# Sample tokens' product of carried state and C: loads and products on GpSimd over the next group, row sums of 1024 columns on VectorE

## The chip, the cores and the metric

The kernel runs on one core of a Trainium2 chip. The core has a matrix engine (TensorE, PE in the profile; PEld is its loading of weights), VectorE (DVE), ScalarE (ACT), GpSimd (POOL) and SyncE (SP). Each engine runs its own instructions in order and waits for the others by semaphores. DMA transfers are started from an engine's queue, here SP's or GpSimd's. The time is the device time of one execution in microseconds; the three runs shown of the kernel before took 1125.12, 1125.15 and 1128.03 us, median 1125.15.

## The reference

One layer of a hybrid decoder is computed in float32 for two groups of tokens with the same weights: 512 tokens of a prompt, and 8 sample tokens (one new token for each of 8 sequences with a carried state). What matters here is the state-space branch. It has 32 heads of 64 channels, a state of 128 numbers for each channel, and 8 groups of B and C vectors, each shared by 4 heads. For a sample token there is one step of the recurrence:

```
h_new = exp(dt*A) * h_prev + dt * x (outer) B          per head: 64 x 128
y     = h_new . C + D * x                               sum over the 128 state numbers
```

So y needs the product of the carried state `h_prev` and C, summed over the state:

```
(h_prev . C)[b, head, p] = sum_n state_ssm[b, head, p, n] * C[b, group(head), n]
```

for 8 tokens, 2048 channels and 128 state numbers: 2 million products. The rest of y follows from it with a factor and a dot product of B and C. y is gated, normalised and projected together with the prompt's.

## The kernel before, in words

**Tiling.** Activations lie transposed: channels on the 128 partitions, 520 columns (512 prompt tokens, then the 8 sample tokens). A weight tile of 1024 x 128 makes one output tile of 128 x 520, called a column here (`column`, L142). For accuracy each float32 operand is split in a high and a low part, `hi` by ScalarE (L116) and `lo` by VectorE (L117), and each block is multiplied three times (`product`, L124, matmuls on L129). A column's result stands in a pair of PSUM banks, `m`; there are two such pairs, so the column after the next needs the first pair emptied.

**The order of the work.** A list of steps is filled with `todo` and worked off by `perform`; the steps follow one another in the program. TensorE runs its instructions in this order (`manual_schedule` names PE alone). For the other engines and for the DMA queues a planner orders the instructions: among those whose inputs it believes to be ready it takes the one with the earliest place in the program, and what stands under `urgent()` gets a place 300 earlier. The order that it makes is fixed in the program; on the chip each queue is worked off in order.

**The scan.** For each of 8 groups g come four columns (`x0`, `x1`, `bb`, `cc`), each followed by a causal convolution (`conv`, L602): ScalarE copies the product out of PSUM (`xb`, L613) and scales it (`v`, L614), GpSimd does small copies and the sample columns (L615 to L617), VectorE adds three shifted products (`v`, L619), ScalarE takes the tanh (`t`, L620), VectorE makes the result (L621), GpSimd keeps the sample columns (L622). Between the columns, `step(g - 1)` drives the generator `scan` (L637) of the group before: decays (`dec`, `aa`, fetched from DRAM by SP, L634; ScalarE, L648 to L655), transposes and `xdt`, `xde` (L670 to L677), the masked product of C and B (L687 to L693), the chain of states (`hst`, L701 to L714), and two y products of 128 channels (L726 to L732). After the y products come two gate columns (`zz`, `zend`).

**The sample part.** It is the last step of `scan` (L735 to L752). TensorE transposes the group's B and C of the 8 sample tokens (L736), ScalarE copies them out (`bcs`, L738), SP writes them to DRAM (`dbc`, L739). Then, for four tokens at a time, SP loads the carried state (`h0`, called h in the profile: 128 partitions x 4 tokens x 2 halves x 128, L743) and C broadcast to all partitions (`cc`, L744), and VectorE runs eight products with row sums of 128 columns (`jk`, L748), each of which writes one column of `y_s` by its accumulator. `h0`, `cc` and `jk` have one buffer each. The new state itself is made much later, on GpSimd, beside the feed-forward (`sample_state`, L1158).

The step in which the sample part stands comes in group g + 1, after the second gate column of group g (L841), and for group 7 among the pool's columns (`uu`, L908 to L913).

## Time and profile before

| what | value |
|---|---|
| median of three runs | 1125.15 us |
| profiled execution: its own time | 1124.59 us |
| profiled execution: span from first to last instruction | 1122.8 us |
| TensorE busy | 1086.1 us (97%) |
| VectorE busy | 700.6 us (62%) |
| ScalarE busy | 453.1 us (40%) |
| GpSimd busy | 316.0 us (28%) |
| mean granted TensorE clock | 0.991 |
| DMA | 165.34 MB, 147 GB/s in the mean |

How to read the rows: an instruction is named by its line, engine, operation and tiles (`out<-in`), then shapes and a count. In the groups there follow, behind the bar, busy time in us and the mean of one in ns, and then the idle time of that engine just before these instructions, with what ended most of it. In the timeline each row begins with its start and length in us, and square brackets hold the idle time before it and what ended that. Rows of waits give the total in us, how many, and the longest. Rows of DMA issues give the size of one and the median time from issue to landing in us. Wherever a wait is put down to several semaphores, the profile names the last. The ends of matmuls are modelled, so a busy TensorE is not one at its peak.

### The profile page before, as it was taken

How to read it: one execution, taken by the hardware profiler on the slowest of the kernel's cores; microseconds unless marked ns; L12 is line 12 of the kernel's file. 1: busy time of each engine (PE TensorE's matmuls, PEld its weight loads, DVE VectorE, ACT ScalarE, POOL GpSimd, SP SyncE). 2: the span in 40 equal slices, each digit the busy share in tenths (PEclk: the TensorE clock that was granted, in tenths of full speed). 3: DMA queues.
4: the chain of work that ended last, by engine and by line, in shares of the span. 5: the costliest groups of instructions: out<-in, count | busy, mean ns of one | idle time of the engine just before them, and what ended most of it. 6: DMA issues, size and time to landing. Idle time of an engine off the chain costs nothing.

```text
span 1122.8 us, 22179 instructions
## 1 busy us (share of the span) xinstructions
PE 1086.1 (97%) x9222; PEld 1047.7 (93%) x9222; DVE 700.6 (62%) x1195; ACT 453.1 (40%) x734; POOL 316.0 (28%) x482
## 2 busy tenths in 40 slices
PE   8999999999999999999999999999999999999995
PEld 6798989989989899999999999799999999999995
DVE  5677777687686887889677745655566553323332
ACT  3356554645535443665333323542222222222320
POOL 1154223122221221100000000389999950000001
PEclk9999999999999999999999999999999999999998
DMA  9535543445434433554435436266676742223212
GB/s 359 200 99 145 146 128 123 131 147 140 131 130 118 144 109 104 180 171 151 151 132 169 152 125 234 95 196 205 216 215 193 209 166 87 89 87 102 85 53 76
DMA packets 58468, 165.34 MB, mean 147 GB/s; under 512 B 10880, under 2 KB 16512, under 8 KB 57600
## 3 DMA queue, kind: packets, MB, share of 16 engines
q1 hardware_dynamic: 51712, 142.96, 39.1%
q0 software_dynamic: 6656, 20.98, 6.3%
q8 instruction: 72, 1.18, 0.4%
q14 instruction: 28, 0.23, 0.1%
HBM read 151.05 MB, written 12.86 MB: 146 GB/s over the span
## 4 chain that ended last, share of the span: by engine, by line
PE 71%; DMA 11%; DVE 8%; ACT 4%; issue 3%; POOL 2%; SPq 0%; DVEq 0%; ACTq 0%; POOLq 0%
PE m L129 62%; DMA dbc<-bcs 5%; DMA cc<-dbc 4%; PE b L129 4%; DVE v L619 3%; DVE jk L748 1%; PE b L193 1%; ACT whi L116 1%; PE b L286 1%; PE b L726 1%; DVE wlo L117 1%; DMA dec<-dacs 1%; ACT xb L613 1%; POOL hst L713 1%; PE b L728 1%
## 5 line engine op out<-in xcount | busy, mean ns | idle before, releaser
L129 PE MATMUL m<-hh,whi 128*128 128x260 f32 (+1 forms) x1840 | 381.6, 287 | 14.9 <-ACT v L614 13.8
L129 PE MATMUL m<-hl,whi 128*128 128x260 f32 (+1 forms) x1840 | 374.3, 284 | 1.8 <-DVE hl L466 1.6
L129 PE MATMUL m<-hh,wlo 128*128 128x260 f32 (+1 forms) x1840 | 374.4, 284 | 0.0
L116 ACT CAST whi<-raw 128x1024 fp32r<-128x1024 f32 (+2 forms) x169 | 173.0, 1027 | 369.3 <-PE m L129 254.0
L117 DVE TENSOR_TENSOR wlo<-raw,whi 128x1024 fp32r<-128x1024 f32 (+2 forms) x169 | 228.8, 1356 | 145.8 <-ACT whi L116 142.8
L129 PEld LDWEIGHTS m<-hh,whi 128*128 128x128 f32 x1840 | 285.9, 189 | 24.9 <-ACT v L614 17.1
L129 PEld LDWEIGHTS m<-hl,whi 128*128 128x128 f32 x1840 | 285.4, 189 | 2.5 <-DVE hl L466 2.1
L129 PEld LDWEIGHTS m<-hh,wlo 128*128 128x128 f32 x1840 | 285.9, 189 | 0.0
L326 POOL TENSOR_TENSOR r<-me,mhalf 128x5 f32<-128x5 f32 (+2 forms) x6 | 6.4, 1064 | 439.2 <-DVE me L325 439.2
L619 DVE SCALAR_TENSOR_TENSOR v<-xb,cwh,v 128x512 f32<-128x512 f32 x96 | 80.8, 842 | 27.1 <-ACT v L614 26.4
L620 ACT ACTIVATE t<-v 128x520 f32<-128x520 f32 x32 | 20.4, 638 | 114.2 <-DVE v L619 108.3
L1179 DVE TENSOR_TENSOR fs<-m,fs 128x520 f32<-128x520 f32 (+2 forms) x23 | 15.5, 676 | 66.0 <-PE m L129 65.2
L129 PE MATMUL m<-ah,whi 128*128 128x260 f32 x264 | 53.3, 283 | 0.0
L129 PE MATMUL m<-ah,wlo 128*128 128x260 f32 x264 | 53.1, 282 | 0.0
L129 PE MATMUL m<-al,whi 128*128 128x260 f32 x264 | 53.0, 282 | 0.0
L129 PE MATMUL m<-gh,whi 128*128 128x260 f32 x256 | 52.8, 288 | 0.0
L129 PE MATMUL m<-gl,whi 128*128 128x260 f32 x256 | 51.3, 282 | 0.0
L129 PE MATMUL m<-gh,wlo 128*128 128x260 f32 x256 | 51.3, 282 | 0.0
L1168 POOL TENSOR_TENSOR hs<-hs,ht 128x512 f32<-128x512 f32 x32 | 48.5, 1514 | 0.8
L748 DVE SCALAR_TENSOR_TENSOR jk<-h,cc 128x128 f32<-128x128 f32 x128 | 37.1, 290 | 14.8 <-DMA cc<-dbc 13.5
L129 PEld LDWEIGHTS m<-gh,whi 128*128 128x128 f32 x256 | 39.2, 188 | 2.6 <-PE b L286 1.3
L1167 POOL TENSOR_TENSOR hs<-hs,dtx 128x512 f32<-128x512 f32 x32 | 40.7, 1271 | 0.5 <-DMA hs<-in_sssm 0.5
(297 smaller groups left out, 1728.8 us busy)
## 6 DMA issues: line engine op xcount, KB each, us to landing
raw<-in_win SPq DMA_DIRECT2D x73, 512.0 KB, 3.6
raw<-in_wfi SPq DMA_DIRECT2D x44, 512.0 KB, 4.3
araw<-in_wada SPq DMA_DIRECT2D x24, 512.0 KB, 4.1
h<-in_sssm SPq DMA_DIRECT2D x16, 512.0 KB, 4.1
raw<-in_wssd SPq DMA_DIRECT2D x16, 512.0 KB, 3.4
hs<-in_sssm POOLq DMA_DIRECT2D x32, 256.0 KB, 4.2
out_ssms<-hs POOLq DMA_DIRECT2D x32, 256.0 KB, 3.7
raw<-in_wfo SPq DMA_DIRECT2D x16, 512.0 KB, 3.5
```

The lines of the kernel that those rows point to most:

```text
L116: nc.scalar.copy(hi, raw)
L117: nc.vector.tensor_tensor(lo, raw, hi.bitcast(F32), ALU.subtract)
L129: nc.tensor.matmul(o, a[:, k, c0 : c0 + P], b[:, t0:t1], start=f, stop=e)
L193: nc.tensor.matmul(ps[32 * i : 32 * i + 32, 0:n], sc[:, k], raw[:, n * i : n * i + n], start=first, stop=last)
L286: nc.tensor.matmul(ps[32 * i : 32 * i + 32, 0:256], scr[:, k], w[:, 256 * i : 256 * i + 256], start=k == 0 and j == 0, stop=k == KD - 1 an ...
L613: nc.scalar.copy(shape(xb[:, 3 + t0 : 3 + t1]), o)
L619: nc.vector.scalar_tensor_tensor(v[:, 0:TP], xb[:, k : k + TP], w(k), v[:, 0:TP], ALU.mult, ALU.add)
L620: nc.scalar.activation(t, v, AF.Tanh, bias=0.0, scale=1.0)
L748: nc.vector.scalar_tensor_tensor(jk, h0[:, i, j], 1.0, cc[:, i], ALU.mult, ALU.mult, accum_out=y_s[:, 2 * g + j, b + i : b + i + 1],)
L1167: nc.gpsimd.tensor_tensor(h, h, at(dtx[:, 1]), ALU.mult)
L1168: nc.gpsimd.tensor_tensor(h, h, t, ALU.add)
L1179: nc.vector.tensor_tensor(view(s[:, t0:t1]), u, view(s[:, t0:t1]), ALU.mult)
```

## The change

The sample part leaves the generator `scan` and becomes one of its own, `sample(g)`, with four parts. Part 1 transposes and copies out as before; `dbc` is written from GpSimd's queue. Part 2 loads state and C for the first four tokens, from GpSimd's queue. Part 3 multiplies them on GpSimd, in place, as one product of 128 x 1024, sums the rows on VectorE in one instruction with 8 sums of 128 columns, and loads the second four. Part 4 multiplies and sums those. `h0` and `cc` keep one buffer each, and `jk` is gone.

Part 1 of group g stands where the whole sample part stood. Parts 2, 3 and 4 come in the next group of the loop after the columns `x0`, `bb` and `cc`. Groups 6 and 7 follow among the pool's columns. The arithmetic and the bytes moved stay the same.

```diff
-        nc.sync.dma_start(out=dbc[g].rearrange("a b n -> (a b) n"), in_=bcs)
-        for b in range(0, NS, 4):
-            h0 = sp.tile([P, 4, 2, P], F32, tag="h0", name=f"h0_{g}_{b}")
-            cc = sp.tile([P, 4, P], F32, tag="cc", name=f"cc_{g}_{b}")
-            nc.sync.dma_start(out=h0, in_=I["sssm"][g, :, b : b + 4])
-            nc.sync.dma_start(out=cc, in_=dbc[g, 1, b : b + 4].unsqueeze(0).broadcast_to([P, 4, P]))
-            jk = sp.tile([P, P], F32, tag="jk", name=f"jk_{g}_{b}")
-            for i in range(4):
-                for j in range(2):
-                    nc.vector.scalar_tensor_tensor(
-                        jk, h0[:, i, j], 1.0, cc[:, i], ALU.mult, ALU.mult,
-                        accum_out=y_s[:, 2 * g + j, b + i : b + i + 1],
-                    )
...
+    def sample(g):
+        sp = S["sp"]
+        def loads(b):
+            h0 = sp.tile([P, 4, 2, P], F32, tag="h0", name=f"h0_{g}_{b}")
+            cc = sp.tile([P, 4, P], F32, tag="cc", name=f"cc_{g}_{b}")
+            nc.gpsimd.dma_start(out=h0, in_=I["sssm"][g, :, b : b + 4])
+            nc.gpsimd.dma_start(out=cc, in_=dbc[g, 1, b : b + 4].unsqueeze(0).broadcast_to([P, 4, P]))
+            return h0, cc
+        def sums(b, h0, cc):
+            nc.gpsimd.tensor_tensor(h0, h0, cc.unsqueeze(2).broadcast_to([P, 4, 2, P]), ALU.mult)
+            out = y_s[:, 2 * g : 2 * g + 2, b : b + 4].rearrange("p j b -> p b j")
+            nc.vector.tensor_reduce(out, h0, axis=AX.X, op=ALU.add)
+        tb = bank()
+        nc.tensor.transpose(tb[0:16, 0:P], bc_s[:, g].rearrange("p a b -> p (a b)"), ident)
+        bcs = sp.tile([16, P], F32, tag="bcs", name=f"bcs{g}")
+        nc.scalar.copy(bcs, tb[0:16, 0:P])
+        nc.gpsimd.dma_start(out=dbc[g].rearrange("a b n -> (a b) n"), in_=bcs)
         yield
+        got = loads(0)
+        yield
+        sums(0, *got)
+        got = loads(4)
+        yield
+        sums(4, *got)
...
+    def part(g):
+        def fn():
+            if g not in samples:
+                samples[g] = sample(g)
+            next(samples[g], None)
+        return fn
...
             if g and (g, fn) != (1, x0) and (g == 1 or fn is not cc):
                 todo(step(g - 1))
+            if g > 1 and fn is not x1:
+                todo(part(g - 2))
...
             todo(zz(2 * g - 1), ZZ(2 * g - 1))
             todo(step(g - 1))
-            todo(step(g - 1))
+            todo(part(g - 1))
             todo(zend(2 * g - 1))
...
         todo(uu(t), UU(t))
-        if t != 3:
+        if t != 3 and t < 6:
             todo(step(7))
+        if t < 3:
+            todo(part(6))
+        elif t > 4:
+            todo(part(7))
...
     todo(wpool(3), I["wpool"][3])
+    todo(part(7))
```

## The prediction

> **What bounds the kernel now.** I read the page's busy times first, then its chain of waits, then TensorE's waits by stage, and last the timeline of one group of the scan.

> ```profile
> span 1122.8 us, 22179 instructions
> PE 1086.1 (97%) x9222; PEld 1047.7 (93%) x9222; DVE 700.6 (62%) x1195; ACT 453.1 (40%) x734; POOL 316.0 (28%) x482
> PE 71%; DMA 11%; DVE 8%; ACT 4%; issue 3%; POOL 2%; SPq 0%; DVEq 0%; ACTq 0%; POOLq 0%
> PE m L129 62%; DMA dbc<-bcs 5%; DMA cc<-dbc 4%; PE b L129 4%; DVE v L619 3%; DVE jk L748 1%; PE b L193 1%; ACT whi L116 1%; PE b L286 1%; PE b L726 1%; DVE wlo L117 1%; DMA dec<-dacs 1%; ACT xb L613 1%; POOL hst L713 1%; PE b L728 1%
> ```

> TensorE is idle for 1122.8 - 1086.1 = 36.7 us, and the change touches none of its instructions, so all that it can win lies in those idle spans. The two transfers of the sample tokens (dbc, cc) make up 9% of the chain. That is not 9% to be won: the chain runs backwards through whatever released the next step, and TensorE works beside most of it. The waits of TensorE itself say how much is at stake. The windows show the scan of groups 0 to 6 (115 to 387 us) and the columns behind it; their columns are busy time of PE, PEld, DVE, ACT, POOL, then clock, DMA share, GB/s.

> ```profile
> 115.00:387.00 272.00, 258.98 (x2247) 252.09 (x2247) 205.95 (x442) 139.07 (x254) 68.33 (x166) 0.99 0.44 134
> 387.00:478.00 91.00, 91.00 (x801) 89.61 (x800) 74.41 (x195) 46.34 (x83) 16.10 (x30) 1.00 0.39 131
> PE m L129 <- ACT v L614: 12.9, 10, 2.7
> ```

> In the scan TensorE is idle for 272.00 - 258.98 = 13.0 us, and 12.9 us of it, ten waits, are for ScalarE to empty a product's PSUM pair. From 387 us on it waits for nothing. So the stake is 12.9 us, about 2.15 us in each of six groups of some 45 us. Why is ScalarE late? One group (times from the span's start):

> ```profile
> 206.55 0.38 SPq L634 DMA_DIRECT2D dec<-dacs  x1
> 208.87 0.87 SPq L739 DMA_DIRECT2D dbc<-bcs  x1
> 213.61 1.29 DVE L675 TENSOR_TENSOR xdt<-b,tok 128x512 f32<-128x512 f32 x2 [2.10 <-PE b L670]
> 216.32 0.23 ACT L648 ACTIVATE cd<-dec 128x16 f32<-128x16 f32 x1 [3.96 <-DMA dec<-dacs]
> 217.72 0.33 SPq L744 DMA_DIRECT2D cc<-dbc  x1
> 218.26 0.58 ACT L613 COPY xb<-m 128x520 f32<-128x520 f32 x1
> 219.18 1.04 POOL L677 TENSOR_TENSOR xde<-xdt,tok 128x512 f32<-128x512 f32 x1
> 219.56 1.21 DVE L619 SCALAR_TENSOR_TENSOR v<-xb,cwh,v 128x512 f32<-128x512 f32 x1 [4.66 <-ACT v L614]
> 220.93 0.29 DVE L748 SCALAR_TENSOR_TENSOR jk<-h,cc 128x128 f32<-128x128 f32 x1 [0.17 <-DMA cc<-dbc]
> 224.00 0.64 ACT L620 ACTIVATE t<-v 128x520 f32<-128x520 f32 x1 [1.88 <-DVE v L619]
> 226.70 1.89 PE L701 MATMUL b<-xde,bm 128*128 128x256 f32 x8
> 231.01 0.29 DVE L748 SCALAR_TENSOR_TENSOR jk<-h,cc 128x128 f32<-128x128 f32 x1 [0.47 <-DMA cc<-dbc]
> 231.23 0.75 DVE L619 SCALAR_TENSOR_TENSOR v<-xb,cwh,v 128x512 f32<-128x512 f32 x1
> 232.07 0.64 ACT L620 ACTIVATE t<-v 128x520 f32<-128x520 f32 x1 [5.31 <-DVE v L619]
> 233.55 0.59 ACT L613 COPY xb<-m 128x520 f32<-128x520 f32 x1
> 234.87 0.51 PE L129 MATMUL m<-hh,whi 128*128 128x260 f32 x2 [0.53 <-ACT v L614]
> 243.77 0.51 PE L129 MATMUL m<-hh,whi 128*128 128x260 f32 x2 [1.18 <-ACT v L614]
> ```

> The group is a loop. The decay table (dec) is fetched again when the second y product has freed its buffer (206.55); ScalarE stands before it until 216.32, and only then empties x0's product (218.26). From there each convolution hangs on the one before it: three v sums on VectorE, the tanh on ScalarE (224.00, 232.07), and behind the tanh in ScalarE's queue the copy of the next product. TensorE stands twice, 0.53 and 1.18 us, because that file comes late. The row products (jk) sit in VectorE's queue between the v sums, and those for the second four tokens wait there for cc, with a v sum behind them (231.01, 231.23).

> **The change, part by part.** First what leaves VectorE, six groups together, by the rows for 115 to 387 us:

> ```profile
> L748 DVE SCALAR_TENSOR_TENSOR jk<-h,cc 128x128 f32<-128x128 f32 x96 | 27.7, 288 | 11.3 <-DMA cc<-dbc 10.3
> ACT whi L116 <- PE m L129: 8.0, 6, 1.3
> ```

> Removed: 96 products of 288 ns, 27.7 us, and 10.3 us of waits for cc: 38.0 us, or 6.3 us a group. (Their accumulator reads run beside the next instruction.) SP loses five transfers a group; the weight loads behind them gain nothing that counts, since ScalarE's high part of the weights (whi) waits here for TensorE and not for a load: zero, and no bound beyond, as the loads only come earlier.

> Added on VectorE: two row sums of 1024 columns a group. The nearest rows are the pool's row sums, with few columns:

> ```profile
> L885 DVE TENSOR_REDUCE red<-spl 128x8 f32<-128x128 f32 x2 | 0.6, 280 | 0.1
> L885 DVE TENSOR_REDUCE red<-spl 128x8 f32<-128x32 f32 x2 | 0.4, 178 | 0.1
> ```

> (280 - 178) / 96 = 1.06 ns a column, so 280 + 896 x 1.06 = 1230 ns. As bounds I take 1.0 us (no fixed part beyond these) and 1.6 us. Twelve of them are 14.8 us.

> Added on GpSimd: two products of 128x1024 a group, and the issue of five transfers. What they cost VectorE is the unknown of this change. No product of that width is in the trace; the rows are 128x512 products, and VectorE's low part of the weights (wlo) beside a GpSimd that multiplies without a break (749 to 900 us) and after it has ended (910 to 1070 us; the row of fs is of that stretch too):

> ```profile
> L677 POOL TENSOR_TENSOR xde<-xdt,tok 128x512 f32<-128x512 f32 x14 | 14.6, 1044 | 39.2 <-DVE xdt L675 39.2
> L117 DVE TENSOR_TENSOR wlo<-raw,whi 128x1024 fp32r<-128x1024 f32 x26 | 54.3, 2090 | 27.6 <-ACT whi L116 26.1
> L117 DVE TENSOR_TENSOR wlo<-raw,whi 128x1024 fp32r<-128x1024 f32 x23 | 28.8, 1251 | 67.1 <-ACT whi L116 66.3
> L1179 DVE TENSOR_TENSOR fs<-m,fs 128x520 f32<-128x520 f32 x7 | 4.9, 700 | 26.0 <-PE m L129 26.0
> L1155 POOL DMA_DIRECT2D bb<-dbc x32 | 18.7, 585 | 0.0
> L1155 POOL DMA_DIRECT2D bb<-dbc x32: 546/587/592, 733.4 to 902.0; - x32
> ```

> A new product is two of the first, 2.1 us. A VectorE instruction took 2090 - 1251 = 0.84 us longer beside a 128x512 product, so 1.7 us beside one of twice the width. The group above shows the same: the v sum at 219.56 took 1.21 us in place of 0.75, and ended 0.55 us after xde did. Bounds: nothing, if the product falls where VectorE waits for others, and 2.1 us, if it takes its whole length from it. I take 1.7 us, because VectorE is busy for 205.95 of 272 us, mostly on instructions of this kind. Twelve are 20.4 us.

> [...]

> On GpSimd itself a group gains 2 x 2.1 + 5 x 0.585 = 7.1 us on 68.33 / 6 = 11.4 of 45 us, off the path by its amount. Its queue matters more. The load of cc now waits in it until dbc has landed. Behind it stands xde, which the state product needs only at 226.70. Even if dbc took the 8.4 us of its row below, cc would go out at 208.87 + 8.4 = 217.3 and both halves of xde would be done by 219.4: free, with 7 us to spare. On VectorE each row sum waits for its product; behind it stand v sums, for which the tanh waits, so there a late product costs what it is late. The second four tokens use the same buffers: their loads wait in GpSimd's queue for the first row sum. The code's spreading sets only priorities here; the planner starts what is ready (bb above was issued from 733.4 to 902.0 us, though by the code its last calls come with the last of the feed-forward's columns, seven of which end after 910 us, by the row of fs). So I expect the first product just behind x0's small GpSimd work, at about 221 us of the group shown, among x0's v sums.

> Moved traffic, by its rows:

> ```profile
> dec<-dacs SPq DMA_DIRECT2D x4, 1024.0 KB, 9.3
> cc<-dbc SPq DMA_DIRECT2D x16, 256.0 KB, 3.9
> h<-in_sssm SPq DMA_DIRECT2D x16, 512.0 KB, 4.1
> dbc<-bcs SPq DMA_DIRECT2D x8, 8.0 KB, 8.4
> 206.00:216.50 10.50, 10.50 (x102) 10.33 (x99) 6.79 (x10) 6.16 (x18) 1.23 (x2) 1.00 0.61 193
> ```

> dbc took 8.4 us because on SP's queue it stands behind dec. From GpSimd it can pass dec; then cc's 256 KB cross while dec is still coming, and 256 KB at 193 GB/s are 1.4 us, for which ScalarE stands longer at 216.32. Bounds 0 and 1.4 us a group; I take half, 0.7, or 4.2 us in six groups, as nothing tells when cc will be issued.

> Groups 6 and 7 of the sample work fall in 387 to 478 us, where TensorE waits for nothing with VectorE busy for 74.41 of 91 us: zero, hidden by that slack; if it is gone, two groups at the net below.

> **Sum.** VectorE: -38.0 + 14.8 + 20.4 = -2.8 us; dec: +4.2 us; together +1.4 us over the six groups, or 0.2 us a group on a loop that is 2.15 us too long. The profiled execution has 1124.59 us (its span and 1.8 us around it), 0.6 below the median of 1125.15. 1124.6 + 1.4 = 1126.0 us: no difference that can be measured (0.3%, 3.4 us, is about what a measurement of this kernel can tell). From end to end of the bounds the sum runs from -38.0 + 12 = -26, cut off at the -12.9 that TensorE waits, to -38.0 + 19.2 + 25.2 + 8.4 = +14.8 us.

> **Rivals.** *The idle time of VectorE takes the work.* It stands for 2.10 and 4.66 us a group before xdt and the first v sum. If dbc lands quickly and the planner puts the first product there, the product and its sum cost nothing, and from the loop go the jk between v sums and the wait at 231. For it: 6.8 us of idle time against 3.3 us of work. Against: jk, with the same inputs, was placed after the first v sum. Some 2 of 2.15 us a group close in five of six groups, less one for what the second product costs: -9 us, 1116 us.

> *GpSimd's queue becomes the bound.* The second loads go out after the first row sum (about 226.5), land 4.1 us later, and the product runs from about 231.5 to 233.6, or later by each microsecond that the first sum slips. Behind it in order stand the small copies and the sum for the sample columns of the next convolution, whose tanh waits for them. It decides once the product starts after that convolution's product is copied out (233.55): then about 3 us a group come on top, 18 us in six, 1143 us. For it: the loads' place behind a row sum that has the lowest priority on VectorE. Against: in the group shown there are 2 us to spare.

> *A product takes its whole length from VectorE,* and none falls in idle time: 25.2 in place of 20.4 us, +4.8, so 1124.6 + 6.2 = 1130.8 us, slower. [...]

> **Chances.** Forecast, 1126 us within 1121 to 1128: 0.35. Idle time, 1112 to 1121: 0.33. Queue, 1132 to 1145: 0.19. Whole length, 1128 to 1132: 0.13. Hence faster 0.33, same 0.35, slower 0.32. The range 1114 to 1137 leaves out the ends of the first and second rival, about 0.1 each.

> **What will show it.** Right: TensorE's waits for ScalarE's v between 9 and 17 us in the scan, the first v sums of x0 stretched to 2 us beside a product of 2.1 us, row sums of 1.2 us, cd still waiting 4 us or more for dec. The idle-time rival: those waits fall to under 5 us and the first product lies ahead of x0's first v sum. The queue rival: GpSimd's small copies wait behind the product, and TensorE's waits exceed 25 us. What would make it wrong from the start: a row sum well over 1.6 us, or new waits of TensorE after 387 us.

## The result, and the profile after

The changed kernel takes 1178.15 us (median of 4 runs, 1174.61 to 1183.33) where the kernel before took 1125.13 us beside it: a ratio of 1.0475, with a 95% interval of 1.0449 to 1.0501. It is 53 us slower, and the predicted 1126 us and the whole predicted range missed it. The profiled execution has 1174.61 us.

The page of the kernel after, busy times and one line of the 40 slices (the granted TensorE clock in tenths):

```profile
span 1172.8 us, 21965 instructions
PE 1104.5 (94%) x9222; PEld 1065.1 (91%) x9222; DVE 685.3 (58%) x955; ACT 453.6 (39%) x734; POOL 377.3 (32%) x538
PEclk9999989989898989999999999999999999999998
```

The span is 50.0 us longer, and it divides into two parts of a different kind. TensorE stands still for 1172.8 - 1104.5 = 68.3 us where it was 36.7, so 31.6 us more. And the same 9222 matmuls keep it busy for 1104.5 us where it was 1086.1, so 18.4 us more. The second part is a slower clock: five of the slices over the scan show an 8 (80 to 90% of full speed; a 9 stands for 90% or more), and the windows say the same. The stages are the scan of groups 0 to 6, the columns behind it, and the rest; the columns are again busy time of PE, PEld, DVE, ACT, POOL, then clock, DMA share and GB/s. The second block is the scan of the kernel before.

```profile
113.00:430.00 317.00, 274.41 (x2239) 265.98 (x2238) 195.78 (x260) 139.06 (x254) 111.61 (x207) 0.92 0.37 114
430.00:525.00 95.00, 90.62 (x774) 89.09 (x773) 69.61 (x135) 44.13 (x79) 30.66 (x45) 0.98 0.37 123
525.00:1172.80 647.80, 636.73 (x5418) 619.88 (x5416) 342.99 (x421) 216.17 (x299) 198.92 (x225) 0.99 0.45 146
```

```profile
113.00:387.00 274.00, 260.98 (x2264) 254.09 (x2264) 207.92 (x444) 139.98 (x255) 68.43 (x167) 0.99 0.44 133
```

The scan took 274 us before (113 to 387) and takes 317 us now, which is 43 of the 50 us; the next stage grew from 91 to 95 us. VectorE, which the change was to relieve, is busy for less time in the scan than before (195.78 us, it was 207.92), and the kernel is slower all the same. So the time is in waits. The waits of the kernel after (total, times, longest), and behind them one of the kernel before:

```profile
ACT t L620 <- DVE v L619: 153.0, 27, 8.9
DVE y_s L749 <- POOL h L747: 84.7, 14, 8.9
POOL cc L743 <- DMA dbc<-bcs: 51.0, 8, 8.3
PE m L129 <- ACT v L614: 43.6, 14, 5.2
```

```profile
DVE v L619 <- ACT v L614: 26.4, 6, 4.9
```

The two new kinds of work, by line (busy time, mean of one in ns, then the idle time ahead of them):

```profile
L747 POOL TENSOR_TENSOR h<-h,cc 128x1024 f32<-128x1024 f32 x16 | 38.6, 2411 | 49.8 <-DMA h<-in_sssm 26.1 <-DMA cc<-dbc 23.7
L749 DVE TENSOR_REDUCE y_s<-h 128x8 f32<-128x1024 f32 x16 | 19.5, 1221 | 84.7 <-POOL h L747 84.7
```

They are to be read as one chain. GpSimd waits 51.0 us for dbc before it issues the load of cc, and 49.8 us more for the loads before it multiplies. VectorE waits 84.7 us for the products, in front of the row sums. Not all of that is new: before, it stood 26.4 us in front of x0's first v sums, until ScalarE had their input ready. ScalarE's tanh waits for v sums, and TensorE waits 43.6 us for ScalarE where it was 13.8 in the whole span. One group shows how the links hang together (times from the span's start):

```profile
222.34 0.38 SPq L634 DMA_DIRECT2D dec<-dacs  x1
224.92 0.55 POOL L755 DMA_DIRECT2D dbc<-bcs  x1 [0.69 <-ACT bcs L754]
233.00 0.79 ACT L614 ACTIVATE v<-m,cwh 128x520 f32<-128x520 f32 x1
233.14 0.57 POOL L743 DMA_DIRECT2D cc<-dbc  x1 [7.67 <-DMA dbc<-bcs]
236.75 2.40 POOL L747 TENSOR_TENSOR h<-h,cc 128x1024 f32<-128x1024 f32 x1 [3.04 <-DMA cc<-dbc]
239.18 1.22 DVE L749 TENSOR_REDUCE y_s<-h 128x8 f32<-128x1024 f32 x1 [8.49 <-POOL h L747]
240.32 2.44 DVE L619 SCALAR_TENSOR_TENSOR v<-xb,cwh,v 128x512 f32<-128x512 f32 x2
244.65 0.64 ACT L620 ACTIVATE t<-v 128x520 f32<-128x520 f32 x1 [8.27 <-DVE v L619]
247.45 0.51 PE L129 MATMUL m<-hh,whi 128*128 128x260 f32 x2 [3.07 <-ACT v L614]
247.99 2.37 POOL L747 TENSOR_TENSOR h<-h,cc 128x1024 f32<-128x1024 f32 x1 [3.21 <-DMA h<-in_sssm]
250.39 1.22 DVE L749 TENSOR_REDUCE y_s<-h 128x8 f32<-128x1024 f32 x1 [4.37 <-POOL h L747]
258.82 0.80 PE L129 MATMUL m<-hh,whi 128*128 128x260 f32 x2 [3.83 <-ACT v L614]
```

The input of x0's v sums is complete at 233.00 + 0.79 = 233.8. They start at 240.32, because the row sum of the first four tokens stands in front of them in VectorE's order, and its product ends only at 239.15. TensorE then stands for 3.07 us. The second half repeats it: the row sum at 250.39 stands ahead of x1's v sums, and TensorE stands for 3.83 us. Before, the small products (jk) stood behind the first v sum, at 220.93, so a late cc held up only what came after it.

What follows the gap is the other part of the loss. The windows behind the first of these two gaps:

```profile
248.22:251.63 3.41, 3.41 (x18) 3.41 (x17) 1.24 (x2) 0.00 (x0) 2.53 (x4) 0.50 0.03 11
251.63:255.00 3.37, 3.36 (x28) 3.15 (x27) 3.37 (x5) 0.00 (x0) 0.87 (x2) 1.00 0.44 124
```

For 3.41 us the granted clock is 0.50, and TensorE gets through 18 matmuls in place of 28. The clock record of the trace has 11 such falls, of 3.41 or 6.83 us, between 108 and 515 us; before there were two in the scan, and one at 24 us. TensorE works 46.5 us within these eleven falls and worked 9.8 us within the three of before. Half of the difference is 18.4 us, and that accounts for the growth in busy time.

### The profile page after: what moved, and what is told of

The parts are those of the page before. It is cut to its first block, busy times and chain, and to the rows that moved or that the text cites. A ratio compares the mean times of both kernels' runs of the same rounds, so it can differ in the third digit from the quotient of the medians.

```text
span 1172.8 us, 21965 instructions
## 1 busy us (share of the span) xinstructions
PE 1104.5 (94%) x9222; PEld 1065.1 (91%) x9222; DVE 685.3 (58%) x955; ACT 453.6 (39%) x734; POOL 377.3 (32%) x538
## 3 DMA queue, kind: packets, MB, share of 16 engines
q8 instruction: 72, 1.18, 0.4%
## 4 chain that ended last, share of the span: by engine, by line
PE 69%; DMA 11%; POOL 7%; DVE 5%; issue 4%; ACT 3%; SPq 0%; POOLq 0%; ACTq 0%; DVEq 0%
PE m L129 61%; DMA dbc<-bcs 4%; PE b L129 4%; DMA h<-in_sssm 3%; POOL h L747 3%; DMA cc<-dbc 2%; DVE v L619 2%; PE b L726 1%; PE b L193 1%; POOL xde L677 1%; ACT whi L116 1%; DVE wlo L117 1%; PE b L286 1%; PE b L728 1%; DMA dec<-dacs 1%
## 5 line engine op out<-in xcount | busy, mean ns | idle before, releaser
L129 PE MATMUL m<-hh,whi 128*128 128x260 f32 (+1 forms) x1840 | 388.6, 292 | 44.6 <-ACT v L614 43.6
L129 PE MATMUL m<-hl,whi 128*128 128x260 f32 (+1 forms) x1840 | 380.8, 288 | 1.8 <-DVE hl L466 1.6
L129 PE MATMUL m<-hh,wlo 128*128 128x260 f32 (+1 forms) x1840 | 379.9, 287 | 1.3 <-DVE wlo L117 1.3
L129 PEld LDWEIGHTS m<-hh,whi 128*128 128x128 f32 x1840 | 292.6, 194 | 56.1 <-ACT v L614 48.1
L117 DVE TENSOR_TENSOR wlo<-raw,whi 128x1024 fp32r<-128x1024 f32 (+2 forms) x169 | 229.7, 1361 | 155.6 <-ACT whi L116 152.8
L116 ACT CAST whi<-raw 128x1024 fp32r<-128x1024 f32 (+2 forms) x169 | 173.0, 1027 | 362.6 <-PE m L129 248.6
L129 PEld LDWEIGHTS m<-hl,whi 128*128 128x128 f32 x1840 | 292.6, 194 | 2.5 <-DVE hl L466 2.1
L129 PEld LDWEIGHTS m<-hh,wlo 128*128 128x128 f32 x1840 | 291.9, 193 | 1.5 <-DVE wlo L117 1.5
L620 ACT ACTIVATE t<-v 128x520 f32<-128x520 f32 x32 | 20.4, 637 | 159.1 <-DVE v L619 153.0
L619 DVE SCALAR_TENSOR_TENSOR v<-xb,cwh,v 128x512 f32<-128x512 f32 x96 | 79.4, 827 | 0.9
L749 DVE TENSOR_REDUCE y_s<-h 128x8 f32<-128x1024 f32 x16 | 19.5, 1221 | 84.7 <-POOL h L747 84.7
L747 POOL TENSOR_TENSOR h<-h,cc 128x1024 f32<-128x1024 f32 x16 | 38.6, 2411 | 49.8 <-DMA h<-in_sssm 26.1
L129 PE MATMUL m<-ah,whi 128*128 128x260 f32 x264 | 53.2, 283 | 0.0
L129 PE MATMUL m<-ah,wlo 128*128 128x260 f32 x264 | 53.1, 282 | 0.0
L129 PE MATMUL m<-al,whi 128*128 128x260 f32 x264 | 53.0, 282 | 0.0
L129 PE MATMUL m<-gh,whi 128*128 128x260 f32 x256 | 52.8, 288 | 0.0
L129 PE MATMUL m<-gl,whi 128*128 128x260 f32 x256 | 51.3, 282 | 0.0
L129 PE MATMUL m<-gh,wlo 128*128 128x260 f32 x256 | 51.3, 282 | 0.0
L1191 POOL TENSOR_TENSOR ht<-bb,xds 128x512 f32<-128x512 f32 x32 | 48.0, 1499 | 2.4 <-DMA bb<-dbc 1.9
L1193 POOL TENSOR_TENSOR hs<-hs,ht 128x512 f32<-128x512 f32 x32 | 43.3, 1354 | 0.8
## 6 DMA issues: line engine op xcount, KB each, us to landing
raw<-in_win SPq DMA_DIRECT2D x73, 512.0 KB, 4.1
raw<-in_wfi SPq DMA_DIRECT2D x44, 512.0 KB, 4.4
araw<-in_wada SPq DMA_DIRECT2D x24, 512.0 KB, 4.0
h<-in_sssm POOLq DMA_DIRECT2D x16, 512.0 KB, 4.7
raw<-in_wssd SPq DMA_DIRECT2D x16, 512.0 KB, 3.4
hs<-in_sssm POOLq DMA_DIRECT2D x32, 256.0 KB, 4.1
out_ssms<-hs POOLq DMA_DIRECT2D x32, 256.0 KB, 2.9
raw<-in_wfo SPq DMA_DIRECT2D x16, 512.0 KB, 3.5
```

Of the source, the lines that this page charges most:

```text
L116: nc.scalar.copy(hi, raw)
L117: nc.vector.tensor_tensor(lo, raw, hi.bitcast(F32), ALU.subtract)
L129: nc.tensor.matmul(o, a[:, k, c0 : c0 + P], b[:, t0:t1], start=f, stop=e)
L619: nc.vector.scalar_tensor_tensor(v[:, 0:TP], xb[:, k : k + TP], w(k), v[:, 0:TP], ALU.mult, ALU.add)
L620: nc.scalar.activation(t, v, AF.Tanh, bias=0.0, scale=1.0)
L747: nc.gpsimd.tensor_tensor(h0, h0, cc.unsqueeze(2).broadcast_to([P, 4, 2, P]), ALU.mult)
```

## The experiments

Three theories were put against each other. *Order*: the loss comes from what stands, in the order fixed for VectorE, behind a row sum that waits for a late product. *Product*: it comes from the product on GpSimd itself, which takes its time from VectorE's instructions beside it (in the kernel before a low part of the weights, wlo, took 2.09 us in the mean beside GpSimd's products and 1.25 us after they had ended). *Queue*: it comes from the transfers on GpSimd's queue, where the load of cc waits for dbc with all that stands behind it.

### Both halves kept at the program's place

```diff
-            nc.gpsimd.tensor_tensor(h0, h0, cc.unsqueeze(2).broadcast_to([P, 4, 2, P]), ALU.mult)
+            tc.keep_in_program_order(nc.gpsimd.tensor_tensor(h0, h0, cc.unsqueeze(2).broadcast_to([P, 4, 2, P]), ALU.mult))
...
-            nc.vector.tensor_reduce(out, h0, axis=AX.X, op=ALU.add)
+            tc.keep_in_program_order(nc.vector.tensor_reduce(out, h0, axis=AX.X, op=ALU.add))
```

> The changed kernel with the product and the row sum of each four tokens tied to their place in the program (behind what stands before them on GpSimd and on VectorE), so behind bb's states and behind cc. Theory order (the time went to the row sum ahead of x0's v sums on VectorE and the product ahead of x0's copies on GpSimd, both waiting for dbc and cc): VectorE's wait at the row sum falls from 84.7 us to under 10, TensorE's waits for ScalarE's v in the scan from 43 us to 13 or less, the time to 1112 to 1128 us. Theory product (a product of 2.4 us on GpSimd shuts VectorE out): the products are still there, TensorE's waits stay over 30 us and the time over 1150 us. Theory queue (transfers on GpSimd's queue block it): cc still waits 51 us for dbc there, the time stays over 1145 us.

Measured: 1133.09 us, 1.0091 [1.0057, 1.0125] of before. Its waits:

```profile
POOL cc L743 <- DMA dbc<-bcs: 53.6, 8, 8.1
DVE y_s L749 <- POOL h L747: 29.5, 13, 2.6
PE m L129 <- DVE gz L772: 16.9, 6, 3.2
```

The row sum that is left in the way, in the timeline of a group:

```profile
255.34 1.22 DVE L749 TENSOR_REDUCE y_s<-h 128x8 f32<-128x1024 f32 x1 [2.61 <-POOL h L747]
256.48 0.69 DVE L772 SCALAR_TENSOR_TENSOR gz<-zt,m 128x520 f32<-128x520 f32 x1
```

The load of cc waits as long for dbc as in the kernel after (53.6 us), and yet 45 of the 53 us are gone. So that wait by itself makes at most the 8 us that are left, and the order makes the rest. This run ties GpSimd's products and VectorE's row sums together, so it doesn't tell the order of one engine from that of the other. The order theory missed its own numbers (under 10 us at the row sums, 1112 to 1128 us), and the other two missed theirs by more. What remains has a place too: the second row sum now stands ahead of a gate's product (gz), for which TensorE waits 16.9 us.

### One half kept

The first run keeps the first four tokens' product and sum, the second (with b == 4) those of the second four.

```diff
-            nc.gpsimd.tensor_tensor(h0, h0, cc.unsqueeze(2).broadcast_to([P, 4, 2, P]), ALU.mult)
+            m = nc.gpsimd.tensor_tensor(h0, h0, cc.unsqueeze(2).broadcast_to([P, 4, 2, P]), ALU.mult)
+            if b == 0:
+                tc.keep_in_program_order(m)
...
-            nc.vector.tensor_reduce(out, h0, axis=AX.X, op=ALU.add)
+            r = nc.vector.tensor_reduce(out, h0, axis=AX.X, op=ALU.add)
+            if b == 0:
+                tc.keep_in_program_order(r)
```

> The kernel after, with only the first four tokens' product and row sum of each group kept at the place that the program gives them (behind the state product of the group); the second four's are left where the planner puts them. Order theory (the loss is what stands in order behind a row sum that waits for a late product: x0's v sums behind the first, x1's low part and v sums behind the second): the waits of 8 us for the first product go, those for the second stay or move to the gate columns; about half of the 50 us remain to be lost: 1140 to 1158 us. Product theory (the loss is the product's time on GpSimd, which shuts VectorE out): nothing is taken away, 1165 to 1180 us. Queue theory (GpSimd's queue, held by the load of cc that waits for dbc, makes all behind it late): the load keeps its wait of about 6 us a group, so 1165 to 1180 us as well.

> The kernel after, with only the second four tokens' product and row sum of each group kept at the place that the program gives them; the first four's stay where the planner puts them, ahead of x0's v sums. Order theory: VectorE's waits of 8 us for the first product stay, the 4 us waits ahead of x1's v sums go; 1145 to 1165 us, and together with the run that keeps the first alone the two losses taken away make up about the 45 us that keeping both took away. Product theory: 1165 to 1180 us. If this run stays within 5 us of the kernel after, and the other one takes nearly all, the first row sum alone makes the loss.

Measured: 1136.18 us (1.0099 [1.0073, 1.0126]) with the first half kept, 1149.39 us (1.0224 [1.0200, 1.0247]) with the second. The waits with the second half kept:

```profile
DVE y_s L751 <- POOL h L747: 83.5, 14, 11.2
PE m L129 <- ACT v L614: 29.9, 9, 4.8
```

Here the first row sum stands ahead of x0's v sums as in the kernel after, and the kernel is 24 us over before. The second row sum stands ahead of gz, but TensorE waits only 0.5 us for gz here, so the 24 us are the first half's. The second half's place ahead of x1's v sums then makes the other 29 us, by difference (1178.15 - 1149.39). VectorE's waits in total are as long as in the kernel after (83.5 and 84.7 us), since the first row sum waits longer here (up to 11.2 us): what counts is what stands behind a wait. With the first half kept nearly all was won, not half as expected: in that kernel the second row sum does not stand ahead of x1's v sums any more, but behind the v sums of the group's last column, with a gate's gz behind it, as in the run with both kept. So the two runs do not add up (42 and 29 us won, 45 together), and what the second half costs was read from the other run. The 1149 us lie in the order theory's range and the 1136 us 4 us under it; the other theories had 1165 to 1180 us.

### The product on VectorE

```diff
-            nc.gpsimd.tensor_tensor(h0, h0, cc.unsqueeze(2).broadcast_to([P, 4, 2, P]), ALU.mult)
+            nc.vector.tensor_tensor(h0, h0, cc.unsqueeze(2).broadcast_to([P, 4, 2, P]), ALU.mult)
```

> The changed kernel with the two products of a group on VectorE instead of GpSimd, transfers still from GpSimd's queue. Theory order: the product waits for cc on VectorE itself, ahead of all v sums but none of x0's small copies on GpSimd: VectorE's waits before product and sum 50 to 70 us, the time 1145 to 1170 us. Theory product: no product on GpSimd, so the loss goes, 1120 to 1130 us. Theory queue: GpSimd still waits 51 us for dbc, 1150 to 1178 us.

Measured: 1120.85 us, 0.9972 [0.9953, 0.9992] of before: just faster than before. The product theory's range (1120 to 1130 us) holds this time, and those of the order and the queue theory don't. Two rows of its waits:

```profile
DVE h L747 <- DMA cc<-dbc: 44.1, 7, 7.7
PE m L129 <- ACT v L614: 13.0, 7, 3.0
```

One group of its timeline:

```profile
222.48 1.23 DVE L747 TENSOR_TENSOR h<-h,cc 128x1024 f32<-128x1024 f32 x1 [6.37 <-DMA cc<-dbc]
223.62 0.74 DVE L619 SCALAR_TENSOR_TENSOR v<-xb,cwh,v 128x512 f32<-128x512 f32 x1
```

The order theory as first put misses here. VectorE still waits 44.1 us, now in front of the product, and the product stands ahead of x0's first v sum. What differs is how much lies between cc's landing and the v sum: the product starts at 222.48 and the v sum at 223.62, 1.1 us later, where in the kernel after 3.57 us pass (236.75 to 240.32): 2.4 us of product on GpSimd and 1.2 us of row sum. The second half's product and sum stand behind bb's v sums, where their loads have long landed. So order and product work together: the product on GpSimd makes late what the order puts in front. That is read from the timeline; the second half's place is another one too, so this run doesn't separate the two.

### The transfers on SP's queue, the product on GpSimd

```diff
-            nc.gpsimd.dma_start(out=h0, in_=I["sssm"][g, :, b : b + 4])
+            nc.sync.dma_start(out=h0, in_=I["sssm"][g, :, b : b + 4])
```

The loads of cc and the transfer of dbc are moved in the same way.

> The changed kernel with the five transfers of a group back on SP's queue; products on GpSimd, row sums on VectorE. In its fixed order the first row sum stands behind x0's v sums and the second behind bb's. Theory order: VectorE's wait at the row sums falls to under 30 us, the time to 1125 to 1140 us. Theory product: as slow as the changed kernel, 1160 to 1180 us. Theory queue: GpSimd no longer waits for dbc, so 1125 to 1140 us too; from theory order it differs by GpSimd's own waits before the product, 0 to 15 us by queue, over 20 us by order.

Measured: 1130.37 us, 1.0056 [1.0037, 1.0076] of before. The order came out different here: the first row sum behind x0's three v sums, the second behind bb's. VectorE then waits only 8.9 us for the products. The order and the queue theory both expected 1125 to 1140 us, and the product theory's 1160 to 1180 us are missed. GpSimd's own waits ahead of the products are 40.4 us, where the order theory named over 20 and the queue theory under 15. A product now runs beside v sums and weights instead of ahead of them. This shows its price, in the timeline and in a mean. First the timeline:

```profile
219.67 2.94 POOL L747 TENSOR_TENSOR h<-h,cc 128x1024 f32<-128x1024 f32 x1
220.27 3.43 DVE L117 TENSOR_TENSOR wlo<-raw,whi 128x1024 fp32r<-128x1024 f32 x1
```

And in the mean of all v sums, 931 ns where the run below has 799:

```profile
L619 DVE SCALAR_TENSOR_TENSOR v<-xb,cwh,v 128x512 f32<-128x512 f32 x96 | 89.4, 931 | 27.9 <-ACT v L614 27.0
```

The low part of the weights (wlo), 1.22 us in the mean in the scan of the kernel before and of the kernel after, takes 3.43 us beside a product of 2.94 us: it began 0.60 us after the product and ended 1.09 us after it. VectorE's work outside the sample tokens can be taken from the busy times: 711.0 us less 19.4 of row sums is 691.6 here, and 704.0 less 20.3 of products and 19.4 of sums is 664.3 us in the run below, where nothing of it is on GpSimd. The difference is 27.3 us for 16 products, 1.71 us each. In the kernel after the same difference is 685.3 - 19.5 = 665.8 us: there the products stretch VectorE's work by next to nothing, since it mostly stands still and waits for them.

### Product on VectorE and transfers on SP's queue

The two edits above together. Of the change there remain the wide product, the row sum and the spreading over the next group.

```diff
-            nc.gpsimd.dma_start(out=h0, in_=I["sssm"][g, :, b : b + 4])
+            nc.sync.dma_start(out=h0, in_=I["sssm"][g, :, b : b + 4])
...
-            nc.gpsimd.tensor_tensor(h0, h0, cc.unsqueeze(2).broadcast_to([P, 4, 2, P]), ALU.mult)
+            nc.vector.tensor_tensor(h0, h0, cc.unsqueeze(2).broadcast_to([P, 4, 2, P]), ALU.mult)
```

> The kernel after with the products on VectorE and the five transfers on SP's queue: of the change there remain the wide row sums, one wide product in place of eight small ones with their sums, and the parts spread over the next group. Order theory: the row sum never waits for another engine, but the product waits for cc on VectorE, behind dec; 1115 to 1127 us. Product theory: GpSimd has none of the product, so 1115 to 1127 us too. Queue theory: GpSimd's queue is as before the change, so it is faster than the run with the products on VectorE and the transfers on GpSimd (1120.9 us) by what TensorE still waited there for late v sums, some 10 us: 1110 to 1116 us.

Measured: 1111.19 us, 0.9887 [0.9867, 0.9906] of before, the fastest of all versions. The queue theory's range (1110 to 1116 us) holds this time; the other two expected 1115 to 1127 us. Waits:

```profile
PE m L129 <- ACT v L614: 4.8, 5, 1.5
DVE h L747 <- DMA cc<-dbc: 1.8, 3, 1.3
```

The window of the scan of groups 0 to 6, and the first product of one group in the timeline:

```profile
113.00:370.00 257.00, 252.95 (x2230) 247.48 (x2230) 203.46 (x271) 138.28 (x251) 83.57 (x163) 1.00 0.48 137
```

```profile
213.93 1.21 DVE L619 SCALAR_TENSOR_TENSOR v<-xb,cwh,v 128x512 f32<-128x512 f32 x1 [3.57 <-ACT v L614]
215.34 1.23 DVE L747 TENSOR_TENSOR h<-h,cc 128x1024 f32<-128x1024 f32 x1 [0.20 <-DMA cc<-dbc]
```

TensorE's waits for ScalarE fall from 13.8 to 4.8 us, no gap exceeds 1.5 us in the scan and the clock stays at 1.00. VectorE waits 1.8 us for cc, where it was 44.1 with the transfers on GpSimd's queue, because the first product here stands behind x0's first v sum (213.93, then 215.34). What the queue itself does and what the order does isn't separated by these two runs: both changed. The run further down that holds the order, with the product on GpSimd, tests the queue by itself. Of the four combinations the products on GpSimd cost 19 us more than on VectorE with SP's queue (1130.4 and 1111.2) and 57 us more with GpSimd's (1178.2 and 1120.9).

### The wide forms alone

The kernel before, with nothing spread and the loads on SP's queue as they were:

```diff
-            for i in range(4):
-                for j in range(2):
-                    nc.vector.scalar_tensor_tensor(
-                        jk, h0[:, i, j], 1.0, cc[:, i], ALU.mult, ALU.mult,
-                        accum_out=y_s[:, 2 * g + j, b + i : b + i + 1],
-                    )
+            nc.vector.tensor_tensor(h0, h0, cc.unsqueeze(2).broadcast_to([P, 4, 2, P]), ALU.mult)
+            out = y_s[:, 2 * g : 2 * g + 2, b : b + 4].rearrange("p j b -> p b j")
+            nc.vector.tensor_reduce(out, h0, axis=AX.X, op=ALU.add)
```

> The kernel before with only the form of VectorE's work changed: in place of eight products of 128 columns with their sums, one product of 1024 columns and one row sum for each four tokens; all still in the piece of the group where it was, the loads on SP's queue, nothing spread over the next group. It tells apart what the wide forms and what the spreading bring in the fastest kernel so far (1111.2 us). VectorE has 2.31 us for each half before (eight of 288 ns) and 2.48 us in the wide forms, so by their own time they are worth nothing. If the spreading makes the gain: 1122 to 1130 us. If the wide forms make it (fewer instructions for the planner to put between v sums): 1109 to 1115 us.

Measured: 1116.85 us, 0.9922 [0.9900, 0.9945] of before, between the two ranges. So the wide forms bring some 8 of the 13.9 us, though by their own time they bring nothing: a product takes 1.226 and a row sum 1.214 us. The gain looks to lie in the order again:

```profile
ACT t L620 <- DVE v L619: 97.2, 27, 5.6
```

The tanh waits 97.2 us for v sums where it was 108.3; there are two pieces of sample work among the v sums of a convolution and not eight. TensorE's waits for ScalarE's v fall to 1.5 us. No run changes the number of pieces alone, so this is read and not tested. That the spreading makes the other 5 us isn't shown beyond the two medians, whose intervals touch. In the profiled executions most of the difference is TensorE's busy time (1087.3 and 1081.9 us) and not its waits.

### The sample work issued earlier

```diff
+            todo(part(g - 1))
             todo(zz(2 * g - 2), ZZ(2 * g - 2))
...
-            todo(part(g - 1))
             todo(zend(2 * g - 1))
```

> The changed kernel with the first part (transpose, copy, dbc) of group g - 1 ahead of both gate columns instead of behind them, so that dbc crosses before the decay table is fetched. Theory order: dbc lands in 2 to 4 us in place of 8, product and sum fall among the gate columns, VectorE's wait at the row sums is under 25 us, the time 1112 to 1130 us. Theory product: sixteen products of 2.4 us stay, over 1150 us. Theory queue: GpSimd waits for dbc some 20 us in place of 51, 1135 to 1155 us.

Measured: 1144.58 us, 1.0190 [1.0162, 1.0218] of before. That is in the queue theory's range (1135 to 1155 us); the order theory's (1112 to 1130 us) and the product theory's (over 1150 us) miss. dbc lands quickly (2.9 us in the median, 7.8 in the kernel after), and GpSimd's wait for it falls from 51.0 to 14.4 us, but VectorE's wait for the products hardly falls:

```profile
DVE y_s L749 <- POOL h L747: 78.1, 16, 8.7
POOL h L747 <- DMA h<-in_sssm: 61.2, 8, 10.8
```

The loads for the second half now go out while dec is under way, and the second product waits up to 10.8 us for them. The same was tried on the fastest version, with products on VectorE and transfers on SP's queue, and the piece put one column earlier still:

```diff
             if g > 1 and fn is not x1:
                 todo(part(g - 2))
+            if g and fn is bb:
+                todo(part(g - 1))
...
-            todo(part(g - 1))
             todo(zend(2 * g - 1))
```

> The same with the transfer of the sample rows to DRAM and the first loads issued one column earlier, ahead of the group's gate columns, while dec is not in flight. If dbc's landing behind dec is what makes cc late (8 us beside dec, 2 to 4 us without it), then the load of cc waits under 4 us, VectorE's product waits under 2 us for cc, TensorE's waits in the scan fall from 13 to under 6 us: 1110 to 1118 us. If dbc's landing is off the path once the products stand on VectorE, the time is that of the run without the earlier issue, within 4 us.

Measured: 1136.86 us, 1.0104 [1.0087, 1.0122] of before, and 26 us behind the fastest version. Neither expectation held: not 1110 to 1118 us, and not the fastest version's time within 4 us.

```profile
DVE h L747 <- DMA cc<-dbc: 23.1, 8, 4.1
PE m L129 <- ACT v L614: 15.1, 6, 3.3
```

dbc lands in 3.2 us, as expected, and VectorE waits 23.1 us for cc, where it was 1.8. A shorter transfer did not help, because the product moved forward with it: it now stands in front of the v sums of the columns ahead of the gates, 4 us before its data. ScalarE's waits for dec grew as well, from 29.5 to 49.2 us; whether that is a cause or follows from the rest isn't separated. In this kernel the length of a transfer isn't what counts but the distance between its landing and the place of its first reader.

### Product on GpSimd, transfers on SP's queue, kept at the program's place

```diff
-            nc.gpsimd.dma_start(out=h0, in_=I["sssm"][g, :, b : b + 4])
+            nc.sync.dma_start(out=h0, in_=I["sssm"][g, :, b : b + 4])
...
-            nc.vector.tensor_reduce(out, h0, axis=AX.X, op=ALU.add)
+            tc.keep_in_program_order(m)
+            tc.keep_in_program_order(nc.vector.tensor_reduce(out, h0, axis=AX.X, op=ALU.add))
```

Here m is the product on GpSimd.

> The kernel after with the five transfers on SP's queue and the products on GpSimd, products and row sums kept at the place that the program gives them. What is left of the change's cost here is the product on GpSimd itself with its hand over to VectorE. Order theory: no row sum stands ahead of a v sum that is ready, so TensorE's waits in the scan are at most the 15 us of before: 1112 to 1126 us. Product theory (it takes its 2.4 us from VectorE, 16 times): 20 to 38 us above the run with the products on VectorE and the transfers on SP's queue, 1131 to 1149 us. Queue theory: what the transfers on GpSimd's queue cost is what this run is faster than the one with both kept and the transfers on GpSimd's queue (1133.1 us): 5 to 15 us.

Measured: 1133.87 us, 1.0074 [1.0048, 1.0100] of before.

```profile
DVE y_s L750 <- POOL h L747: 27.6, 12, 2.6
PE m L129 <- DVE gz L773: 15.0, 6, 3.2
```

The same as with the transfers on GpSimd's queue (1133.09 us), so with the order held and the product on GpSimd the queue costs nothing that can be measured, where the queue theory expected 5 to 15 us. With the product on VectorE no run holds the order, so there the queue by itself stays untested. The order theory missed its range (1112 to 1126 us) as well: it overlooked that the second row sum stands here ahead of gz. The product theory's range holds the time, but not by its reason: VectorE's other work is 686.7 - 19.5 = 667.2 us, 2.9 us over the fastest version. What the traces show is the wait for the product: in each of the six groups the second row sum waits 2.6 us for it ahead of gz, and TensorE waits for gz six times, 15.0 us in all.

### The half clock, by stops of TensorE made on purpose

Twelve stops in the feed-forward of the kernel before, in a stretch where TensorE hardly waits otherwise; the copies leave the values as they are. The long stops have 320 in place of 96.

```diff
+            if 3 <= j < 15:
+                nc.scalar.copy(G["hh"][:, :, 0:96], G["hh"][:, :, 0:96].bitcast(F32))
             pg = column([wg], xh, xl)
```

> The kernel before, where nothing of the sample tokens' work is touched; ahead of each of twelve gate columns of the feed-forward (the fourth to the fifteenth, all in a stretch in which TensorE otherwise never waits) ScalarE copies 768 columns of the normed input's high part onto themselves, so that TensorE must stand still from the end of the column before until the copy is done, by estimate from ScalarE's rows 1 to 1.5 us each time. Both theories of the clock expect the stops alone: 12 to 18 us more than before, 1137 to 1144 us, TensorE's busy time as before, and a granted clock of 1.00 in that stretch.

> The same with 2560 columns in each copy, so stops of some 2.5 to 3.2 us. If a stop of TensorE longer than about 2.2 us is what brings the granted clock down to half for a few microseconds afterwards, TensorE's busy time grows too, by 1.5 to 3 us for each of the twelve stops beside the idle time of 30 to 38 us: 1172 to 1195 us, with the clock under 0.95 in that stretch. If the half clock in the scan has another cause (what the other engines draw there), only the idle time is added: 1155 to 1163 us with a clock of 1.00.

Measured: 1148.78 us (1.0212 [1.0186, 1.0237]) with the short stops and 1179.32 us (1.0481 [1.0453, 1.0509]) with the long ones. The window of that stretch in the kernel before, with short stops and with long ones, the last with one of the falls:

```profile
690.00:950.00 260.00, 259.40 (x2117) 251.97 (x2116) 141.53 (x143) 83.32 (x127) 189.69 (x218) 1.00 0.56 174
```

```profile
690.00:950.00 260.00, 239.06 (x1923) 229.16 (x1922) 123.63 (x135) 85.25 (x131) 184.76 (x218) 1.00 0.54 165
```

```profile
690.00:950.00 260.00, 221.01 (x1659) 211.10 (x1658) 114.17 (x124) 95.12 (x121) 180.60 (x218) 0.94 0.49 153
763.65:767.06 3.41, 3.41 (x16) 3.41 (x17) 0.70 (x1) 0.36 (x1) 3.37 (x5) 0.50 0.94 310
```

TensorE's waits for the copies, with short stops and with long ones:

```profile
PE m L129 <- ACT hh L1202: 20.1, 12, 1.7
```

```profile
PE m L129 <- ACT hh L1202: 38.0, 12, 3.2
```

Twelve stops of 1.68 us cost 20.1 us of idle time and leave the clock at 1.00; the busy time over the span is 1085.5 us, as before (1086.1). Twelve stops of 3.17 us cost 38.0 us, and TensorE's busy time is 1100.5 us, 15.0 us above the run with short stops. The clock is 0.94 over the 260 us of the stretch: 15.6 us are lost to it, about what nine falls to 0.50 of 3.41 us each make (15.3 us). So a long stop is paid for a second time, and the draw of the other engines in the scan isn't needed for it. The short stops came out above their expected 1137 to 1144 us, mainly since they were longer than the 1 to 1.5 us estimated (20.1 of the 23.9 us); the long ones came out in the range of 1172 to 1195 us that goes with a falling clock.

## Why the prediction was wrong, point by point

**What bounds the kernel** was read rightly: TensorE's waits for ScalarE in the scan. The stake was not complete. All that the change could win was put at those idle spans, 12.9 us, with TensorE's busy time fixed. The fastest version's span is 13.6 us shorter than before (1122.8 and 1109.2), and only 9.4 us of that is idle time (36.7 to 27.3); the other 4.2 us is busy time (1086.1 to 1081.9), mostly since the two falls of the clock in the scan are gone.

**The step that failed is the order of VectorE's instructions.** The prediction put the first product "at about 221 us of the group shown, among x0's v sums". In time that was right: it named 12.1 us after dbc (208.87 to 221), and the product came 11.8 us after it (224.92 to 236.75). But it took it for granted that the planner starts what is ready, as it had placed jk behind the first v sum. The planner fixed the row sum ahead of x0's v sums and the second one ahead of x1's. The sentence "there a late product costs what it is late" stood in the text, with nothing for it in the sum. It is worth 84.7 us of VectorE's waits, where 26.4 us stood at this place before, and TensorE's idle time grew by 31.6 us. Holding both halves at the program's place took away 45 of the 53 us. The sum could not show it, as it netted VectorE's busy time and took the net for the kernel's: that busy time did fall, by 15.3 us (700.6 to 685.3), while the span grew by 50.0 us.

**The 38.0 us removed** held for the 27.7 us of small products. The 10.3 us of waits for cc were not removed but moved: GpSimd took them over (23.7 us for cc, 51.0 for dbc) and handed them on.

**What the products take from VectorE, 20.4 us,** was right in its size and wrong in its place. 1.7 us a product was predicted, and 1.71 us were measured where products meet work; in the kernel after they mostly met an idle VectorE and stretched its work by 665.8 - 664.3 = 1.5 us in all. What they cost there came as waits.

**Row sums and products:** 1.23 us were predicted for a row sum and 1.221 measured, though the line was drawn from rows of 32 and 128 columns out to 1024; 2.1 us for a product and 2.411 measured.

**dbc "can pass dec", and 4.2 us for a later dec:** neither came. dbc was under way 7.8 us in the median, on SP's queue 8.4. ScalarE's waits for dec are 24.3 us in the whole span (14.2 and 10.1 by their two buffers); they were 27.7. The prediction put the 8.4 us down to dbc's place behind dec on SP's queue, and the nearly equal time on GpSimd's queue speaks against that.

**"free, with 7 us to spare" for GpSimd's queue:** free it was, but with less to spare. The profile shows no wait of TensorE for xde, and in the group shown xde ends at 241.4 and its matmuls start at 242.49 us, since the product stands ahead of it on GpSimd. The wait of 53.6 us for dbc makes at most the 8 us that are left with the order kept.

**Zero after 387 us:** wrong by some 4 us. In the stage from 430 to 525 us TensorE waits 4.3 us, 3.0 of them for a gate's product, and the clock is 0.98. The last two row sums stand ahead of the pool's work on VectorE there, with waits of 4.4 and 4.9 us; that these cause TensorE's wait is read from the order and not tested.

**The rivals.** The one that had GpSimd's queue as the bound named the second product, held by loads that go out after the first row sum, and the point from which it decides: the product at 247.99 does start after x1's product is copied out. Its sign, more than 25 us of TensorE's waits, came (43.6 us). But it had the delay go through GpSimd's small copies, and it went through VectorE's order (the tanh at 256.02 waits for VectorE's v sums). It priced this at 18 us in six groups, where the second half makes 29 us; it had nothing for the first half, the other 24 us. The idle-time rival had the place right: the planner did put the first half's row sum ahead of x0's first v sum. The product wasn't ready, so it became a wait of 8.5 us in the group shown. The third rival, a product's whole 2.1 us, isn't borne out by the 1.71 us measured.

**The clock, 18.4 us,** is in no case of the prediction, though the trace of before had two falls of it behind its two longest gaps in the scan (2.69 and 2.37 us). Any gain or loss in idle time was priced at its own length. It is the second term that the sum lacked.

What stays open is why the planner puts the row sum ahead of the v sums with the transfers on GpSimd's queue and behind them with the transfers on SP's. The orders are in the traces, its reasons aren't. A second pair of buffers, so that the second half's loads need not wait for the first row sum, is in no run.

## What to carry to other kernels

Before moving half of a pair of operations to another engine, ask where the other half will stand in its engine's order and what stands behind it: the wait is paid by the first critical instruction behind, whatever the moved work itself costs. Try the plain form first, one wide product and one row sum on the same engine; in this kernel that gained 8 of the 13.9 us that were to be had. And where a trace shows the granted clock fall behind stops of TensorE, count such a stop at more than its length: here twelve stops of 3.17 us cost 38.0 us of idle time and 15.0 us of slower work, twelve of 1.68 us cost 20.1 us of idle time and left the busy time as it was.

## What the runs showed of the hardware

How a gap lay counted too. The eleven falls of the kernel after begin at multiples of 3.413 us from each other (108.27 and 149.23 us are 12 of them apart). In the 3.41 us just ahead of a fall TensorE stood still for 2.33 to 3.41 us in ten of the eleven cases, and for 1.46 us ahead of the fall at 108.27 us; why that was enough, the trace doesn't show. In the scan of before it stood for 2.24 and 2.37 us ahead of the two falls. With both traces divided at the multiples of their own falls, from 30 us on to 20 us before the end, no period at full clock without a fall behind it had TensorE standing for more than 1.57 us. The gap of 2.93 us is cut by the edge at 350.62 us into 1.49 and 1.44 us.

In these runs a small transfer gained next to nothing by another queue while a large one was under way: dbc, 8 KB, took 7.8 us in the median on GpSimd's queue and 8.4 on SP's beside dec of 1024 KB, and about 3 us on either when it was issued earlier (2.9 and 3.2).
